# Layer 1's adaLN gate in two sums with three adding DMAs each, seven places for turned probabilities, and a new written order for the first layer

## The chip, the cores and the metric

The kernel runs on one core of a Trainium2 chip. A core has five engines, each with an instruction queue of its own: TensorE (PE, matrix products, with the loading of its stationary operand shown apart as PEld), VectorE (DVE), ScalarE (ACT), GpSimd (POOL) and SyncE (SP, which here only issues DMAs). The metric is the device time of one execution in microseconds (us). The kernel before took 416.38 us as the median of 3 runs (416.04 to 417.29).

## The reference

A decoder trunk of two layers on one sequence of 256 rows of 1024 numbers, all float32:

```
for i in range(DEPTH):                                   # DEPTH = 2
    shift, scale, gate = split(c @ ada_w[i] + ada_b[i], 3)
    h = rmsnorm(x, norm_g[i]) * (1 + scale) + shift
    y = nsa_mixer(h, ...) if i % 2 == 0 else mlstm_mixer(h, ...)
    x = x + gate * y
return rmsnorm(x, final_g)
```

Layer 1's mixer is sparse attention with 16 heads of 64 in 4 groups. It has a branch on compressed tokens (a small network with a hidden layer and a GELU over blocks of 32 rows), a branch on selected blocks and a sliding window; each has an ALiBi slope, a softmax and a sigmoid gate. With 256 rows there are four blocks of 64 and 16 to be selected, so the selection takes all that are allowed. The sum of the branches is multiplied by SiLU(z), called the path below, and goes through an output projection. Layer 2's mixer is a chunkwise mLSTM with 8 heads. The change is in layer 1 and in the turn from it to layer 2. The gate of layer 1 is one row of 1024 numbers: the 1024 numbers of c times a 1024 x 1024 block of ada_w, plus a third of ada_b.

## The kernel before, in words

Products that need full precision are made of three matmuls: each operand is split into a rounded part (hi, named wh or hh) and the rest (lo, named wl or hl), and hi x hi, hi x lo and lo x hi are added up in a bank of PSUM. ACT makes the hi of a loaded tile (L169), DVE its lo (L174). Loads come as tiles of up to 128 x 1024 in ten places named raw, issued by SP (L86) in a fixed order as soon as a place is free.

Layer 1 has an order of its own. Its first phase (0 to about 53 us) makes the modulated input and the first projections. What follows, to the start of layer 2, is driven by a string of step names, ORDER (L638 to L655): `attention` (L659) runs through the names and calls for each a small function that issues the step's instructions, on whatever engines it needs. Inside this block the scheduler leaves every engine, PE, ACT, DVE, POOL and SP, in the order in which the instructions were issued. So one sequence of names fixes the order on five engines. Layer 2 is ordered by a scheduler of the language, apart from a few stretches.

The names that matter here, with n for a pair of heads or a tile, and the lines of the functions:

- `hi`, `lo`: the two parts of the next weight tile. `k:kk,part`: products for the keys, values and branch gates. `E`: part of the embedding of positions. `hidden:n`: sixteen matmuls of the compression's hidden layer (L597).
- `S:n,a`, `m:n,a`, `e:n,a`, `f:n`: the scores (PE, L795 and L798), their minima with the mask (DVE, L814), the exponentials (ACT, L821) and the scaling factors (DVE, L829).
- `sXY:n,j`: the scaling of the probabilities. X and Y name the engine for each of the two branches: v for DVE, a for ACT, p for POOL. Each branch is two instructions, of 128x256 and 128x128 (L838, on ACT L665).
- `T:n,j,br`, `t:n,j,br`: three transposes of probabilities on PE (L843), and their copy from PSUM to a tile PT by ACT (L665). PT has eight places. `V:n`: the products of values with PT (L860). `C:n`: the compressed branch's products (L865). `y`, `Y`: the product with the path and its parts, into tiles Q. `z:n,q`: a quarter of the path's projection (L1611 to L1613).
- `gp:k`, `ga:k`: the gate's products. The 1024 rows of ada_w's block come as eight raw tiles k = 0 to 7 of 128 rows. `gp:0` (L888) scales tile 0 on ACT by c's numbers into a tile gate; `gp:k` scales tile k in its own place. `ga:0` adds the row of ada_b to gate's first row with a DMA that POOL issues. `ga:k` for k = 1 to 7 (L896) first copies one column of gate to a tile called seen, on POOL, which waits for the DMA before, and then issues a DMA that adds the scaled tile onto gate (L902). After the seven, `gs` (L905) sums gate's 128 rows with four matmuls against a column of ones (L908), `gc` copies the result (ACT), `g4` stores it to DRAM (POOL, L916), and `g5` (L918) reads it back, spread over all 128 rows, into gate (L919).
- `d:s,n`: shift and scale of layer 2, from raw tiles (L886).
- `out:n`, `l:a,half,k`: the output projection. `l` issues the three products of one Q tile with one weight tile, for one row block a and one half of the columns (L925). Three names make nine matmuls.
- `r:a,half`, `rp:a,half`: the residual x + gate * y of a row block and half, with the product on DVE (L1121) and the addition on DVE or POOL (L1122).
- The turn into layer 2, for row block a: `sq` (squares, ACT, L1155), `sc` (inverse root, DVE), `x:a,half` (normalised rows, ACT L1164 or DVE L1162), `tr:a,k4` (four transposes, PE, L1170), `md:a,k4` (scale and shift; the first half on ACT, L1181, the second on DVE, L1179), `ro:a,k4` (the rounded part; the first half on DVE, L1188, the second on ACT, L1186), `re:a,k4` (the rest, DVE, L1192), `n:a,m` (products with layer 2's narrow weights, L1201, one of the three products for each m) and `v:m,n` (products with its first wide weights, L1201). `nh` and `nl` are hi and lo for these.

The dependencies that the string must respect are those of the functions: `tr` needs `x`, `md` needs `tr`, `ro` needs `md`, `n:0,0` needs `ro:0,0` and then `ro:0,1`.

Of the kernel before, what the change touches and what calls it, by code (L numbers as in the profile page):

```python
# [23 lines left out]
class Kernel:  # L24
# [613 lines left out]
    ORDER = """  # L638
    gp:0 hi lo k:0,0 k:0,1 k:0,2 hi k:1,0 k:1,1 k:1,2 k:2,2 lo k:3,2 hi hi lo k:4,2 hi lo lo k:2,1 E:1,0 k:3,1 k:2,0 k:4,1 E:0,0 hi lo k:5,2 k:6,2
    k:3,0 k:4,0 k:5,0 k:6,0 k:7,0 qa:1 qa:3 qb:3 d:0,0 qb:1 hidden:0 gp:1 E:1,1 hi E:0,1 ga:0 hidden:1 ga:1 gp:2 qa:2 qb:2 k:7,2 kd qa:0 k:5,1 G:0  # L640
    qb:0 G:1 vo:0 hi lo hidden:2 lo S:0,0 hidden:3 hi m:0,0 e:0,0 gelu:0 S:0,1 m:0,1 e:0,1 gelu:1 lo z:0,0 gp:3 S:1,0 ga:2 f:0 vo:1 gelu:2 z:0,1
    sap:0,0 S:1,1 m:1,0 k:6,1 d:0,1 k:7,1 hi ga:3 turned z:0,2 vo:2 second m:1,1 T:0,0,1 T:0,0,0 z:0,3 spp:0,1 e:1,0 ckeys e:1,1 t:0,0,0 cvalues:0
    S:2,0 t:0,0,1 cscores:0 lo cscores:1 f:1 spa:1,0 cvalues:1 params d:0,2 zt:0 S:2,1 T:1,0,1 ccopy:0 ccopy:1 ctokens:0 T:0,1,0 t:1,0,1 zo:0 d:0,3 hi
    gp:4 T:0,1,1 t:0,1,1 t:0,1,0 hi z:1,0 z:1,1 ctokens:1 T:1,0,0 m:2,0 e:2,0 t:1,0,0 z:1,2 cdist:0 z:1,3 lo d:1,0 m:2,1 e:2,1 zt:1 cdist:1 cexp ga:4
    spp:1,1 f:2 spp:2,0 S:3,0 zo:1 T:1,1,1 T:1,1,0 gp:5 m:3,0 t:1,1,0 S:3,1 m:3,1 V:0 cprobs t:1,1,1 d:1,1 e:3,0 hi hi cparts:1 cparts:0 V:1 svp:2,1
    S:4,0 S:4,1 T:2,0,0 T:2,0,1 t:2,0,1 t:2,0,0 e:3,1 z:2,0 cturned:0 lo T:2,1,1 T:2,1,0 lo ga:5 z:2,1 t:2,1,1 cpt:0 z:2,2 t:2,1,0 cturned:1 f:3
    spa:3,0 C:0 m:4,0 T:3,0,1 T:3,0,0 m:4,1 z:2,3 e:4,0 e:4,1 t:3,0,0 y:0 V:2 d:1,2 f:4 spp:3,1 T:3,1,0 lo S:5,0 S:5,1 gp:6 ga:6 t:3,0,1 t:3,1,0 hi
    T:3,1,1 t:3,1,1 d:1,3 m:5,0 e:5,0 svp:4,0 zt:2 m:5,1 e:5,1 zo:2 V:3 S:6,0 T:4,0,0 t:4,0,0 T:4,0,1 C:1 S:6,1 y:1 z:3,0 spp:4,1 d:2,0 T:4,1,0
    t:4,0,1 f:5 cpt:1 spv:5,0 T:4,1,1 z:3,1 z:3,2 m:6,0 spv:5,1 m:6,1 t:4,1,0 hi gp:7 t:4,1,1 e:6,0 ga:7 hi lo d:2,1 T:5,0,0 z:3,3 T:5,0,1 V:4 lo C:2
    t:5,0,0 t:5,0,1 S:7,0 T:5,1,1 T:5,1,0 lo Y:0 e:6,1 t:5,1,0 f:6 S:7,1 m:7,0 m:7,1 t:5,1,1 spa:6,0 zt:3 zo:3 Y:1 sap:6,1 hi V:5 out:0 T:6,0,1 d:2,2  # L650
    d:2,3 T:6,1,0 gs out:1 l:1,1,2 d:3,0 e:7,0 e:7,1 f:7 lo l:1,0,2 y:2 t:6,0,1 t:6,1,0 gc d:3,1 T:6,1,1 T:6,0,0 l:0,0,2 d:3,2 l:0,0,3 g4 g5 saa:7,1
    sva:7,0 t:6,0,0 t:6,1,1 hi d:3,3 T:7,1,0 T:7,0,1 lo t:7,1,0 t:7,0,1 hi lo l:0,1,2 T:7,0,0 t:7,0,0 T:7,1,1 t:7,1,1 V:6 V:7 C:3 Y:2 l:0,0,4 l:0,1,3
    y:3 hi l:0,1,4 lo Y:3 hi l:0,1,5 l:0,0,5 l:0,0,6 lo l:0,0,7 l:0,1,6 l:0,1,7 l:1,0,3 nh:3 nl:3 r:0,0 l:1,1,3 l:1,0,4 l:1,1,4 root l:1,0,5 r:0,1
    nh:0 nh:1 sq:0,0 sq:0,1 nl:0 sc:0 x:0,1 nl:1 l:1,0,6 l:1,0,7 rp:1,0 nh:4 x:0,0 tr:0,0 nh:2 md:0,0 tr:0,1 md:0,1 ro:0,1 l:1,1,5 l:1,1,6 l:1,1,7
    ro:0,0 sq:1,0 nl:2 n:0,0 n:0,1 r:1,1 sq:1,1 re:0,0 re:0,1 sc:1 x:1,1 nh:5 nl:4 v:0,0 v:0,1 v:1,0 v:1,1 n:0,2 x:1,0 tr:1,0 md:1,0 tr:1,1 md:1,1  # L655
    v:2,0 v:2,1 ro:1,0 re:1,0 ro:1,1 re:1,1 nl:5 v:0,2 v:1,2 n:1,0 n:1,1 n:1,2 gt:0 gt:1
    """

    def attention(self, blocks):  # L659
# [183 lines left out]
                nc.tensor.transpose(b[:, k * P : k * P + P], st[n][0][j][:, br, k * P : k * P + P], ident)  # L843
# [51 lines left out]

        def gate_add(k):  # L896
            if not k:
                nc.gpsimd.dma_start(self.gate0[0:1], t["ada_b"][0:1, 2048:3072], accum_op=OP.add)
# [2 lines left out]
            nc.gpsimd.tensor_copy(T([P, 1], tag="seen"), self.gate0[:, 0:1])
            nc.gpsimd.dma_start(self.gate0, raw, accum_op=OP.add)  # L902
            self.used.add(n)

        def gate_sum():  # L905
            b = B["gs"] = self.bank(4)
            for j in range(4):
                nc.tensor.matmul(b[32 * j : 32 * j + 32, 0:256], self.ones1.to_broadcast([P, 32]), self.gate0[:, 256 * j : 256 * j + 256], start=True, stop=True, skip_group_check=True, tile_position=(0, 32 * j))  # L908
# [788 lines left out]
```

## Time and profile before

| | us |
|---|---|
| median of 3 timed runs | 416.38 (416.04 to 417.29) |
| profiled execution, its own time | 416.69 |
| its span in the profile | 414.9 |
| time of that execution outside the span | 1.8 |
| granted TensorE clock | 0.998 of full |
| first phase of layer 1 | 0 to about 53 |
| ORDER's stretch | about 53 to 176 |
| rest of layer 2 | 176 to 409 |
| end | 409 to 414.9 |

The profile shows one execution. Its first part gives the busy time of each engine and its share of the span; the chain follows the work that ended last back from the end and says which engine each step of it was on. Views of the trace give busy times in stretches of time (the windows), the instructions in order of time (the timeline, where neighbours of one kind are merged, and where the brackets say how long the engine sat idle before and what ended that), groups of instructions by line and shape, the waits by who waited for whom, and DMAs with the time from issue to landing. Ends of matmuls are modelled, so starts are the surer figures there. "bank" is a bank of PSUM, and "out<-in" names what an instruction writes and reads.

### The profile page before, as it was taken

The page shows a single profiled execution, that of the slowest core. Times are in us where ns is not written, and L with a number is a line of the kernel's source. Part 1 is how long each engine was busy: PE and PEld are TensorE (multiplying, and loading weights), DVE is VectorE, ACT ScalarE, POOL GpSimd, SP SyncE. Part 2 cuts the span into 40 slices and gives each one's busy share as a digit, 9 for nine tenths or more (in the row PEclk, how much of TensorE's full clock was granted, in tenths as well). Part 3 has the DMA queues.
Part 4 walks back from the last instruction along what each step waited for, and adds up shares of the span by engine and source line. Part 5 has one row for each costly group of instructions (what it writes and reads, how often), then busy time and mean ns, then how long its engine had stood idle before and what let it go on. Part 6 is the DMA issues. An engine that isn't in the chain of part 4 may idle for free.

```text
span 414.9 us, 7573 instructions
## 1 busy us (share of the span) xinstructions
PE 406.5 (98%) x2637; PEld 356.5 (86%) x2637; DVE 344.7 (83%) x721; ACT 278.9 (67%) x551; POOL 100.1 (24%) x176
## 2 busy tenths in 40 slices
PE   8999999999999999999999999999999999999994
PEld 5999998889889788888998999888888888888884
DVE  5999899899999989987873799998999766657653
ACT  5666696799999978776549866476366454464522
POOL 4000042286596300155205100001041210220000
PEclk9999999999999999999999999999999999999999
DMA  7999999999897988457684675756956646540002
GB/s 296 413 405 407 399 383 350 321 382 363 216 318 230 326 282 310 149 196 278 191 316 145 205 233 181 296 186 193 343 179 216 209 143 212 173 133 2 0 0 103
DMA packets 28967, 100.47 MB, mean 242 GB/s; under 512 B 3844, under 2 KB 4016, under 8 KB 28800
## 3 DMA queue, kind: packets, MB, share of 16 engines
q1 hardware_dynamic: 26208, 92.30, 62.2%
q0 software_dynamic: 2576, 7.41, 7.8%
q8 instruction: 21, 0.34, 0.3%
q10 hardware_dynamic: 144, 0.26, 0.2%
q14 instruction: 18, 0.15, 0.1%
HBM read 95.15 MB, written 1.13 MB: 232 GB/s over the span
## 4 chain that ended last, share of the span: by engine, by line
PE 92%; DMA 3%; DVE 2%; SPq 1%; ACT 1%; issue 1%; DVEq 0%
PE bank L562 10%; PE bank L564 10%; PE bank L563 10%; PE bank L439 7%; PE bank L1613 6%; PE bank L1611 6%; PE bank L1612 6%; PE bank L925 5%; PE bank L1529 5%; PE bank L1090 5%; PE bank L1201 4%; PE bank L860 3%; PE bank L843 3%; DMA raw<-in_start 3%; PE bank L1403 2%; PE bank L795 2%
## 5 line engine op out<-in xcount | busy, mean ns | idle before, releaser
L174 DVE TENSOR_TENSOR wl<-raw,wh 128x1024 fp32r<-128x1024 f32 (+3 forms) x118 | 138.8, 1192 | 32.8 <-ACT wh L169 30.3
L169 ACT ACTIVATE wh<-raw 128x1024 fp32r<-128x1024 f32 (+4 forms) x118 | 117.5, 1009 | 70.3 <-PE bank L564 31.3
L562 PE MATMUL bank<-wh,one 128*128 128x512 f32 (+2 forms) x208 | 76.9, 370 | 0.0
L563 PE MATMUL bank<-wl,one 128*128 128x512 f32 (+2 forms) x208 | 76.2, 367 | 0.0
L564 PE MATMUL bank<-wh,one 128*128 128x512 f32 (+2 forms) x208 | 76.0, 367 | 0.0
L1611 PE MATMUL bank<-one,wh 128*128 128x256 f32 x208 | 59.5, 286 | 0.0
L1613 PE MATMUL bank<-one,wl 128*128 128x256 f32 x208 | 58.9, 283 | 0.1
L1612 PE MATMUL bank<-one,wh 128*128 128x256 f32 x208 | 58.8, 283 | 0.0
L562 PEld LDWEIGHTS bank<-wh,one 128*128 128x128 f32 x208 | 39.2, 188 | 6.4 <-issue 0.4
L564 PEld LDWEIGHTS bank<-wh,one 128*128 128x128 f32 x208 | 39.2, 188 | 6.2
L563 PEld LDWEIGHTS bank<-wl,one 128*128 128x128 f32 x208 | 39.2, 188 | 5.9
L1613 PEld LDWEIGHTS bank<-one,wl 128*128 128x128 f32 x208 | 39.8, 191 | 0.3 <-DVE wl L174 0.3
L1612 PEld LDWEIGHTS bank<-one,wh 128*128 128x128 f32 x208 | 39.8, 191 | 0.2
L1611 PEld LDWEIGHTS bank<-one,wh 128*128 128x128 f32 x208 | 39.8, 191 | 0.2
L838 POOL TENSOR_SCALAR Pr<-Pr,f 128x128 f32<-128x128 f32 (+1 forms) x38 | 33.0, 923 | 19.8 <-DVE f L829 14.9
L439 PE MATMUL bank<-one,wh 128*128 128x256 f32 x224 | 29.9, 284 | 0.8 <-ACT one L413 0.3
L439 PEld LDWEIGHTS bank<-one,wh 128*128 128x128 f32 x224 | 28.0, 192 | 1.3 <-ACT wh L169 0.8
L821 ACT ACTIVATE Pr<-Pr,mn 128x128 f32<-128x128 f32 (+1 forms) x64 | 28.3, 453 | 0.0
L165 POOL TENSOR_TENSOR raw<-raw,gate 128x256 f32<-128x256 f32 x16 | 13.4, 840 | 53.2 <-DMA raw<-in_out_b 49.2
L1384 DVE SCALAR_TENSOR_TENSOR conv<-bank,one,conv 128x255 f32<-128x255 f32 (+2 forms) x48 | 20.5, 471 | 2.2 <-ACT conv L1379 2.2
L886 DVE CUSTOM_DVE_ANT_0 raw<-raw,one,one 128x1024 f32<-128x1024 f32 x16 | 20.8, 1316 | 0.0
L814 DVE CUSTOM_DVE_ANT_0 Pr<-bank,one 128x128 f32<-128x128 f32 (+1 forms) x64 | 18.7, 352 | 0.2
(351 smaller groups left out, 815.9 us busy)
## 6 DMA issues: line engine op xcount, KB each, us to landing
raw<-in_wide SPq DMA_DIRECT2D x44, 512.0 KB, 4.7
raw<-in_units SPq DMA_DIRECT2D x18, 512.0 KB, 4.4
raw<-in_turn SPq DMA_DIRECT2D x16, 512.0 KB, 7.4
raw<-in_out_b SPq DMA_DIRECT2D x16, 512.0 KB, 3.6
raw<-in_start SPq DMA_DIRECT2D x8, 512.0 KB, 9.6
Q<-in_columns SPq DMA_DIRECT2D x8, 512.0 KB, 9.6
raw<-in_gate SPq DMA_DIRECT2D x8, 512.0 KB, 9.1
raw<-in_hidden SPq DMA_DIRECT2D x8, 512.0 KB, 7.6
```

The costliest lines, as they stand in the source:

```text
L169: self.nc.scalar.activation(v(hi), src, AF.Copy)
L174: (g or self.nc.vector).tensor_tensor(v(lo), src, v(hi).bitcast(F32), op=OP.subtract)
L439: nc.tensor.matmul(out, w[:, ch * P : ch * P + P], h[:, kk], start=(kk == 0 and m == 0 and ch % 2 == 0), stop=(kk == 7 and m == 2), skip_g ...
L562: nc.tensor.matmul(out, self.hh[:, kk, sl], wh, start=first, stop=False, skip_group_check=True)
L563: nc.tensor.matmul(out, self.hh[:, kk, sl], wl, start=False, stop=False, skip_group_check=True)
L564: nc.tensor.matmul(out, self.hl[:, kk, sl], wh, start=False, stop=last, skip_group_check=True)
L821: nc.scalar.activation(v, v, AF.Exp, bias=mn[:, a, br, j : j + 1], scale=-1.0, accum_out=sm[:, a, br, j : j + 1])
L838: es[br].tensor_scalar(v, v, f, None, op0=OP.mult)
L886: nc.vector.tensor_tensor_reduce(raw, raw, self.cbc, scale, self.pca[:, 72 + 8 * b + kc : 73 + 8 * b + kc], OP.mult, OP.add, self.cols1[s] ...
L1611: nc.tensor.matmul(out, wh, self.hh[:, kk], start=first, stop=False, skip_group_check=skip)
L1612: nc.tensor.matmul(out, wh, self.hl[:, kk], start=False, stop=False, skip_group_check=skip)
L1613: nc.tensor.matmul(out, wl, self.hh[:, kk], start=False, stop=last, skip_group_check=skip)
```

## The change

The gate: `gp:0` and `gp:1` scale tiles 0 and 1 into two tiles, gate and a new gate2. Tiles 2 to 7 are added in turn, the even ones onto gate and the odd ones onto gate2, three DMAs each; the seen copy before each reads the sum that is added to. One adding DMA and one seen copy are gone. `gs` sums both tiles into the same bank with two matmuls for each quarter.

Memory: PT has seven places instead of eight. The column of ones and a column called sel become columns of the tile pca, and crep, a repeated copy of c's numbers, shares the place of a tile called zb; layer 2's gate sums read c's numbers from pca instead.

The order: ORDER is written anew from its first name to its last. The same steps stand in it, except that `ga:1` is gone, that one residual addition of the second row block is on POOL instead of DVE (`r:1,1` became `rp:1,1`), and that the letters of the scaling steps differ: of 32 branch scalings 5 were on DVE, 8 on ACT and 19 on POOL, and now 10, 5 and 17. Of the string only the lines with the gate sum and with the first transposes of the turn are shown.

```diff
-        self.sel = self.T(pc, [P, P])
+        self.sel = self.pca[:, 94:95]
...
-        self.ones1 = self.T(self.p1, [P, 1])
+        self.ones1 = self.pca[:, 95:96]
...
-        self.crep = self.T(pc, [P, KC, 32])
+        self.crep = self.T(p1, [P, KC, 32], tag="zb")
...
-    d:2,3 T:6,1,0 gs out:1 l:1,1,2 d:3,0 e:7,0 e:7,1 f:7 lo l:1,0,2 y:2 t:6,0,1 t:6,1,0 gc d:3,1 T:6,1,1 T:6,0,0 l:0,0,2 d:3,2 l:0,0,3 g4 g5 saa:7,1
...
-    nh:0 nh:1 sq:0,0 sq:0,1 nl:0 sc:0 x:0,1 nl:1 l:1,0,6 l:1,0,7 rp:1,0 nh:4 x:0,0 tr:0,0 nh:2 md:0,0 tr:0,1 md:0,1 ro:0,1 l:1,1,5 l:1,1,6 l:1,1,7
-    ro:0,0 sq:1,0 nl:2 n:0,0 n:0,1 r:1,1 sq:1,1 re:0,0 re:0,1 sc:1 x:1,1 nh:5 nl:4 v:0,0 v:0,1 v:1,0 v:1,1 n:0,2 x:1,0 tr:1,0 md:1,0 tr:1,1 md:1,1
...
+    hi V:4 S:7,0 C:2 T:5,0,0 t:5,0,0 zo:3 S:7,1 d:2,3 T:5,1,1 sap:6,1 lo m:7,0 m:7,1 gs t:5,1,1 V:5 T:6,1,1 hi Y:1 hi lo lo e:7,0 spv:6,0 e:7,1 gc g4
...
+    l:1,1,4 l:1,1,5 l:1,0,5 l:1,1,6 nl:2 sq:0,1 sc:0 x:0,0 l:1,1,7 rp:1,1 l:1,0,6 l:1,0,7 x:0,1 rp:1,0 tr:0,0 md:0,0 tr:0,1 md:0,1 ro:0,1 ro:0,0 nl:1
+    n:0,0 re:0,1 sq:1,0 sq:1,1 v:0,0 re:0,0 sc:1 x:1,1 n:0,1 n:0,2 nh:4 nl:4 v:0,1 x:1,0 tr:1,0 md:1,0 tr:1,1 md:1,1 ro:1,1 v:1,0 v:1,1 v:2,0 v:2,1
...
-            pt = PT[n, j, br] = T([P, 384], tag="PT", bufs=8)
+            pt = PT[n, j, br] = T([P, 384], tag="PT", bufs=7)
...
             if not k:
-                raw = self.take_raw(1)[0]
-                copy(self.gate0, raw, scale=self.pca[:, 0:1])
+                W["sums"] = [self.gate0, T([P, D], tag="gate2")]
+            if k < 2:
+                copy(W["sums"][k], self.take_raw(1)[0], scale=self.pca[:, k : k + 1])
                 return
...
-            nc.gpsimd.tensor_copy(T([P, 1], tag="seen"), self.gate0[:, 0:1])
-            nc.gpsimd.dma_start(self.gate0, raw, accum_op=OP.add)
+            nc.gpsimd.tensor_copy(T([P, 1], tag="seen"), W["sums"][k % 2][:, 0:1])
+            nc.gpsimd.dma_start(W["sums"][k % 2], raw, accum_op=OP.add)
...
-            for j in range(4):
-                nc.tensor.matmul(b[32 * j : 32 * j + 32, 0:256], self.ones1.to_broadcast([P, 32]), self.gate0[:, 256 * j : 256 * j + 256], start=True, stop=True, skip_group_check=True, tile_position=(0, 32 * j))
+            for m, w in enumerate(W["sums"]):
+                for j in range(4):
+                    nc.tensor.matmul(b[32 * j : 32 * j + 32, 0:256], self.ones1.to_broadcast([P, 32]), w[:, 256 * j : 256 * j + 256], start=(m == 0), stop=(m == 1), skip_group_check=True, tile_position=(0, 32 * j))
...
-            nc.vector.scalar_tensor_tensor(acc, raws[kc // 2][:, kc % 2], self.crep[:, kc, 0:1], src, op0=OP.mult, op1=OP.add)
+            nc.vector.scalar_tensor_tensor(acc, raws[kc // 2][:, kc % 2], self.pca[:, kc : kc + 1], src, op0=OP.mult, op1=OP.add)
```

More of the change, by code (lines that the diff above doesn't have):

```diff
@@ L638 @@
     ORDER = """
[L639 to L650, printed above, removed]
@@ L651 @@
-    d:2,3 T:6,1,0 gs out:1 l:1,1,2 d:3,0 e:7,0 e:7,1 f:7 lo l:1,0,2 y:2 t:6,0,1 t:6,1,0 gc d:3,1 T:6,1,1 T:6,0,0 l:0,0,2 d:3,2 l:0,0,3 g4 g5 saa:7,1
-    sva:7,0 t:6,0,0 t:6,1,1 hi d:3,3 T:7,1,0 T:7,0,1 lo t:7,1,0 t:7,0,1 hi lo l:0,1,2 T:7,0,0 t:7,0,0 T:7,1,1 t:7,1,1 V:6 V:7 C:3 Y:2 l:0,0,4 l:0,1,3
-    y:3 hi l:0,1,4 lo Y:3 hi l:0,1,5 l:0,0,5 l:0,0,6 lo l:0,0,7 l:0,1,6 l:0,1,7 l:1,0,3 nh:3 nl:3 r:0,0 l:1,1,3 l:1,0,4 l:1,1,4 root l:1,0,5 r:0,1
-    nh:0 nh:1 sq:0,0 sq:0,1 nl:0 sc:0 x:0,1 nl:1 l:1,0,6 l:1,0,7 rp:1,0 nh:4 x:0,0 tr:0,0 nh:2 md:0,0 tr:0,1 md:0,1 ro:0,1 l:1,1,5 l:1,1,6 l:1,1,7
@@ L655 @@
-    ro:0,0 sq:1,0 nl:2 n:0,0 n:0,1 r:1,1 sq:1,1 re:0,0 re:0,1 sc:1 x:1,1 nh:5 nl:4 v:0,0 v:0,1 v:1,0 v:1,1 n:0,2 x:1,0 tr:1,0 md:1,0 tr:1,1 md:1,1
-    v:2,0 v:2,1 ro:1,0 re:1,0 ro:1,1 re:1,1 nl:5 v:0,2 v:1,2 n:1,0 n:1,1 n:1,2 gt:0 gt:1
+    E:0,0 qa:0 hi hi hi gp:0 k:0,1 lo k:0,0 k:0,2 lo E:1,0 k:1,0 k:1,1 ga:0 hi k:1,2 k:2,1 k:2,0 k:3,0 hi k:2,2 k:3,2 lo hi hi lo lo lo lo k:4,0 qa:3
+    k:4,2 k:5,2 k:6,2 k:5,0 qb:3 E:0,1 qa:1 d:0,0 k:7,2 qa:2 k:6,0 gp:1 G:0 E:1,1 G:1 k:3,1 k:7,0 kd hidden:0 hidden:1 hidden:2 hidden:3 gp:3 qb:2
@@ new lines @@
+    qb:0 gp:2 hi qb:1 vo:0 ga:2 vo:1 S:0,0 k:4,1 S:0,1 gelu:0 m:0,0 e:0,0 gelu:1 m:0,1 k:5,1 gelu:2 e:0,1 S:1,0 m:1,0 S:1,1 f:0 e:1,0 lo turned z:0,0
+    m:1,1 d:0,1 ga:3 z:0,1 saa:0,0 T:0,0,0 d:0,2 k:6,1 k:7,1 second ckeys z:0,2 spp:0,1 e:1,1 vo:2 t:0,0,0 hi hi T:0,0,1 t:0,0,1 cscores:0 cscores:1
+    f:1 cvalues:0 lo T:0,1,1 S:2,0 S:2,1 hi cvalues:1 ccopy:1 t:0,1,1 ccopy:0 T:0,1,0 t:0,1,0 d:0,3 z:0,3 hi m:2,0 m:2,1 ctokens:0 ctokens:1 spp:1,1
+    T:1,1,0 zt:0 e:2,0 S:3,0 S:3,1 cdist:0 e:2,1 cdist:1 zo:0 t:1,1,0 cexp gp:4 params lo T:1,1,1 z:1,0 t:1,1,1 f:2 z:1,1 d:1,0 gp:5 cprobs z:1,2
@@ new lines @@
+    spp:1,0 T:1,0,1 T:1,0,0 d:1,1 spv:2,0 t:1,0,0 hi hi ga:4 z:1,3 V:0 spp:2,1 t:1,0,1 V:1 m:3,0 cparts:0 m:3,1 ga:5 T:2,0,1 cparts:1 zt:1 T:2,1,0
+    S:4,0 S:4,1 zo:1 e:3,0 lo t:2,1,0 t:2,0,1 cturned:0 T:2,0,0 e:3,1 T:2,1,1 lo z:2,0 t:2,1,1 f:3 m:4,0 svp:3,0 z:2,1 z:2,2 m:4,1 T:3,0,1 S:5,0 cpt:0
+    e:4,0 C:0 t:2,0,0 e:4,1 T:3,0,0 t:3,0,0 S:5,1 spv:3,1 d:1,2 t:3,0,1 f:4 spv:4,0 z:2,3 gp:7 T:3,1,0 T:3,1,1 gp:6 y:0 lo m:5,0 m:5,1 cturned:1 zt:2
+    V:2 svp:4,1 zo:2 t:3,1,0 d:1,3 t:3,1,1 V:3 lo d:2,0 hi e:5,0 C:1 y:1 T:4,0,1 e:5,1 z:3,0 T:4,0,0 t:4,0,0 S:6,0 t:4,0,1 S:6,1 T:4,1,0 t:4,1,0 ga:6
@@ new lines @@
+    T:4,1,1 t:4,1,1 f:5 sva:5,1 m:6,0 e:6,0 m:6,1 Y:0 d:2,1 d:2,2 z:3,1 z:3,2 ga:7 T:5,1,0 t:5,1,0 cpt:1 e:6,1 f:6 spp:5,0 z:3,3 zt:3 T:5,0,1 t:5,0,1
+    hi V:4 S:7,0 C:2 T:5,0,0 t:5,0,0 zo:3 S:7,1 d:2,3 T:5,1,1 sap:6,1 lo m:7,0 m:7,1 gs t:5,1,1 V:5 T:6,1,1 hi Y:1 hi lo lo e:7,0 spv:6,0 e:7,1 gc g4
+    out:0 T:6,1,0 t:6,1,0 out:1 lo l:0,0,2 f:7 t:6,1,1 d:3,0 svv:7,0 T:6,0,1 g5 t:6,0,1 T:6,0,0 t:6,0,0 y:2 d:3,1 l:0,0,3 sav:7,1 d:3,2 l:0,1,2
+    l:0,1,3 hi hi T:7,0,0 t:7,0,0 T:7,0,1 l:1,1,2 lo t:7,0,1 l:1,0,2 l:1,1,3 lo hi lo T:7,1,0 t:7,1,0 l:1,0,3 T:7,1,1 Y:2 V:6 d:3,3 t:7,1,1 V:7 C:3
@@ new lines @@
+    y:3 nh:3 l:0,1,4 hi lo nh:2 l:1,0,4 Y:3 l:0,1,5 l:0,0,4 l:0,0,5 l:0,0,6 nl:3 l:0,0,7 nh:0 nl:0 nh:1 l:0,1,6 l:0,1,7 root r:0,0 sq:0,0 r:0,1
+    l:1,1,4 l:1,1,5 l:1,0,5 l:1,1,6 nl:2 sq:0,1 sc:0 x:0,0 l:1,1,7 rp:1,1 l:1,0,6 l:1,0,7 x:0,1 rp:1,0 tr:0,0 md:0,0 tr:0,1 md:0,1 ro:0,1 ro:0,0 nl:1
+    n:0,0 re:0,1 sq:1,0 sq:1,1 v:0,0 re:0,0 sc:1 x:1,1 n:0,1 n:0,2 nh:4 nl:4 v:0,1 x:1,0 tr:1,0 md:1,0 tr:1,1 md:1,1 ro:1,1 v:1,0 v:1,1 v:2,0 v:2,1
+    ro:1,0 re:1,0 n:1,0 n:1,1 re:1,1 nh:5 nl:5 n:1,2 gt:0 v:0,2 gt:1 v:1,2
```

## Prediction

> **What bounds the kernel now.** I read the page first: the busy times and the chain that ended last.
>
> ```profile
> PE 406.5 (98%) x2637; PEld 356.5 (86%) x2637; DVE 344.7 (83%) x721; ACT 278.9 (67%) x551; POOL 100.1 (24%) x176
> PE 92%; DMA 3%; DVE 2%; SPq 1%; ACT 1%; issue 1%; DVEq 0%
> ```
>
> TensorE (PE) is busy for 98% of the span and is 92% of the chain. Whatever adds work or idle time to PE lengthens the kernel; whatever shortens another engine does nothing unless PE waits for that engine. An average hides stages, so the next view is the busy time by stage, for the stretch that the change rewrites (53 to 176 us) and the rest of layer 2 behind it. The columns behind the length are PE, PEld, DVE, ACT, POOL, then the granted clock, the DMA share and GB/s.
>
> ```profile
> 53.00:82.00 29.00, 28.88 (x226) 24.96 (x226) 26.05 (x52) 22.15 (x40) 7.87 (x14) 1.00 1.02 349
> 82.00:152.00 70.00, 69.96 (x569) 60.22 (x568) 68.67 (x221) 68.12 (x204) 41.92 (x54) 1.00 0.93 304
> 152.00:176.00 24.00, 23.94 (x138) 19.81 (x135) 21.35 (x45) 18.07 (x34) 1.29 (x1) 1.00 0.68 238
> 176.00:409.00 233.00, 233.00 (x1319) 204.58 (x1320) 181.52 (x323) 135.54 (x217) 40.61 (x71) 1.00 0.55 182
> ```
>
> Two things stand here. PE is full in every stage, and full to the digit from 176 to 409 us, so nothing lost before 176 us can be caught up later. And in 82 to 152 us three engines are nearly full together: PE 69.96, DVE 68.67 and ACT 68.12 of 70 us. Since the ends of matmuls are modelled, small gaps hide in that busy time; the chain, which goes from start to start, shows them (start, length, what, records):
>
> ```profile
> 68.93 3.60 PE bank L597 x32
> ...
> 88.03 0.80 PE bank L843 x6
> ...
> 95.03 0.66 PE bank L843 x6
> ...
> 118.96 0.48 PE bank L843 x3
> ...
> 120.84 0.33 PE bank L843 x3
> ...
> 136.57 1.45 PE bank L860 x16
> 138.03 3.00 PE bank L925 x12
> ...
> 141.68 0.57 PE bank L908 x8
> 142.25 4.40 PE bank L925 x18
> ...
> 154.13 11.12 PE bank L925 x48
> 165.26 0.87 PE bank L1170 x8
> 166.13 2.08 PE bank L925 x9
> 168.21 4.90 PE bank L1201 x32
> 173.11 0.87 PE bank L1170 x8
> 173.98 1.83 PE bank L1201 x8
> ```
>
> An undisturbed run of output products (L925) takes 11.12/48 = 0.232 us each. Eighteen would take 4.17 and took 4.40; twelve would take 2.78 and took 3.00. Three transposes of L843 take 0.33, once 0.48; six take 0.66, once 0.80. These four excesses come to 0.23 + 0.22 + 0.15 + 0.14 = 0.74 us. I allow as much again for runs that I do not quote, 1.5 us in all: that is the most that a better order of the same work could win before 176 us.
>
> **The gate in two sums.** The old gate sum is four matmuls of which the trace has eight records, 0.57 us. The new one has four more of the same shape. On PE at this step before (the L843 are transposed probabilities, gate the sum, the L925 output products):
>
> ```order
> L843 MATMUL bank_428_2113<-one_13_14_87,Pr_386_1934 128x128 [waits Activation_49] x2
> L843 MATMUL bank_428_2113<-one_13_14_87,Pr_386_1934 128x128
> L908 MATMUL bank_429_2117<-gate_165_813,one_22_23_101 32x256 [waits DMASW4_49,DMASW3_49,DVE_49]
> L908 MATMUL bank_429_2117<-gate_165_813,one_22_23_101 32x256 x3
> L925 MATMUL bank_421_2089<-wh_388_1949,Q_207_1052 128x512
> ```
>
> And now, on PE at the same step (gate2 is the second sum, the L860 are head 5's values):
>
> ```order
> L843 MATMUL bank_404_2036<-one_13_14_87,Pr_353_1779 128x128 x2
> L910 MATMUL bank_410_2061<-gate_160_811,one_7_8_72 32x256 [waits DMASW4_49,DMASW1_49,DVE_49]
> L910 MATMUL bank_410_2061<-gate_160_811,one_7_8_72 32x256 x3
> L910 MATMUL bank_410_2061<-gate2_171_828,one_7_8_72 32x256 [waits DMASW2_49]
> L910 MATMUL bank_410_2061<-gate2_171_828,one_7_8_72 32x256 x3
> L860 MATMUL bank_396_2002<-PT_403_2028,one_154_155_808 64x256 [waits Activation_49]
> ```
>
> The two rows with gate2 are new work on the full engine, **+0.57 us**, and the sum has moved ahead of head 5's values. The price is 0.57/8 = 0.071 us per record. The Trainium skill ("TensorE: Matmul & The Clock Gate", Back-to-back issue gap) gives N/2.4 + 2.5 ns between matmuls, 109 ns for 256 columns; by it the addition would be an estimated 0.87 us and the sum 0.3 more. The row decides against that, and the page's Part 3, on small matmuls that overlap in groups of columns, fits the row.
>
> What do the shorter chains of adding DMAs give back? First the time to landing by kind of DMA, then POOL's waits from 53 to 175 us, then the last adding DMA, the write-back and the first use of the gate in order of time:
>
> ```profile
> gate<-raw POOLq DMA_DIRECT2D x7, 512.0 KB, 8.6
> ...
> gate<-whole POOLq DMA_DIRECT2D x1, 512.0 KB, 7.0
> ...
> POOL seen L901 <- DMA gate<-raw: 0.9, 1, 0.9
> ...
> 132.07 0.91 POOL L902 DMA_DIRECT2D gate<-raw  x1 [0.30 <-POOL seen L901]
> ...
> 148.69 0.58 POOL L919 DMA_DIRECT2D gate<-whole  x1 [3.37 <-DMA whole<-adaA]
> 159.05 0.69 DVE L1121 TENSOR_TENSOR y<-bank,gate 128x512 f32<-128x512 f32 x1 [0.17 <-PE bank L925]
> ```
>
> POOL waited 0.9 us in all for an earlier adding DMA, and POOL is not what PE waits for. The last one was issued at 132.07 and landed about 132.98 + 8.6 = 141.6, just as the gate sum started (141.68). The finished gate was written back by about 149.27 + 7.0 = 156.3 and first used at 159.05. So one DMA and one seen copy less, and two chains instead of one, take nothing off PE except what the sum itself waited, 0.2 us at most (it lies in the 1.5 above). In the new order the sum stands ahead of head 5's values, which are the L860 of 136.57 in the chain, so near 136.7; the last product is scaled several steps earlier too, so that I put its adding DMA at 119 to 122 and its landing by 133. I cost the wait at nothing, with some 4 us of margin; if that margin goes, see the rivals.
>
> **The cover that goes.** This is the largest term. In the turn into layer 2, four instructions on other engines stand between the transposes of the new rows (L1170) and the first narrow product (L1201): two that scale and shift, two that round. ACT's half and DVE's half of them in the trace:
>
> ```profile
> 165.73 1.51 ACT L1181 ACTIVATE tz<-bank,cols 128x128 f32<-128x128 f32 x4 [0.71 <-PE bank L1170]
> 167.57 0.63 ACT L1186 ACTIVATE one<-tz 128x512 fp32r<-128x512 f32 x1 [0.33 <-DVE tz L1179]
> ...
> 173.58 1.50 ACT L1181 ACTIVATE tz<-bank,cols 128x128 f32<-128x128 f32 x4 [0.89 <-PE bank L1170]
> ```
>
> ```profile
> 166.17 1.37 DVE L1179 TENSOR_SCALAR tz<-bank,cols 128x128 f32<-128x128 f32 x4 [0.18 <-PE bank L1170]
> 167.45 0.42 DVE L1188 CAST one<-tz 128x512 fp32r<-128x512 f32 x1
> ...
> 175.31 0.41 DVE L1188 CAST one<-tz 128x512 fp32r<-128x512 f32 x1
> ```
>
> The transposes end at 165.26 + 0.87 = 166.13, and DVE's rounding at 167.45 + 0.42 = 167.87. PE cannot start L1201 for 1.74 us, and spent them on nine output products, 2.08 us. What stands on PE at this place before (bank_487 and bank_491 are the transposes, bank_424 the last output products, bank_496 the first narrow product):
>
> ```order
> L1170 MATMUL bank_491_2391<-one_13_14_87,Pr_477_2346 128x128 [waits DVE_49,PE_49]
> L1170 MATMUL bank_491_2391<-one_13_14_87,Pr_477_2346 128x128 x3
> L925 MATMUL bank_424_2092<-wh_455_2227,Q_206_1033 128x512
> L925 MATMUL bank_424_2092<-wl_456_2228,Q_206_1033 128x512
> L925 MATMUL bank_424_2092<-wh_455_2227,Q_206_1033 128x512
> L925 MATMUL bank_424_2092<-KL_425_2093,Q_194_986 128x512 x3
> L925 MATMUL bank_424_2092<-KH_426_2094,Q_194_986 128x512 x3
> L1201 MATMUL bank_496_2419<-wh_472_2337,one_3_4_70 128x272 [waits DVE_49,PE_49]
> ```
>
> And now (line numbers are two higher):
>
> ```order
> L927 MATMUL bank_424_2118<-KL_426_2120,Q_193_944 128x512 x3
> L927 MATMUL bank_424_2118<-KH_427_2121,Q_193_944 128x512 x3
> L1172 MATMUL bank_482_2388<-one_13_14_87,Pr_473_2340 128x128 [waits Activation_49]
> L1172 MATMUL bank_482_2388<-one_13_14_87,Pr_473_2340 128x128 x3
> L1172 MATMUL bank_484_2398<-one_13_14_87,Pr_475_2359 128x128 [waits DVE_49,PE_49]
> L1172 MATMUL bank_484_2398<-one_13_14_87,Pr_475_2359 128x128 x3
> L1203 MATMUL bank_489_2417<-wh_465_2320,one_3_4_70 128x272 [waits DVE_49,PE_49]
> ```
>
> All output products now stand ahead of the transposes, and nothing is between these and L1203. The nine products are not saved, only done earlier, so PE idles for the 1.74 us and a little for the signal: **+1.8 us**, bounds 1.7 (the rows above) and 2.4 (if a residual multiplication of 0.69 us, the 159.05 row, now stands just ahead of DVE's half). Queued behind the waiting product on PE is the whole of layer 2. At the second row block the cover stays: between its transposes (173.11 + 0.87 = 173.98) and DVE's rounding (175.31 + 0.41 = 175.72) lie 1.74 us, before with eight L1201 in 1.83 us, now with eight too (four steps). No cost there.
>
> **The rest of the new order.** Every row from 53 to 176 us changes its place; most of that has one answer, that PE does the same work in another sequence. Changes of kind between fp32 products (transposes and the like) and rounded ones rise by two round trips. The 18 and 12 products above cost 0.23 and 0.22 more than their rate, behind such a change; other runs show nothing: 0 to 0.46 us for two, I take **+0.2**. The scaling steps move between engines. One unit is a row of 128x256 and one of 128x128; grouped by shape:
>
> ```profile
> L838 POOL TENSOR_SCALAR Pr<-Pr,f 128x256 f32<-128x256 f32 x19 | 20.2, 1063 | 0.0
> L838 POOL TENSOR_SCALAR Pr<-Pr,f 128x128 f32<-128x128 f32 x19 | 14.9, 784 | 19.8 <-DVE f L829 14.9 <-ACT PT L665 3.6 <-ACT tz L756 1.3
> ...
> L665 ACT ACTIVATE Pr<-Pr,f 128x256 f32<-128x256 f32 x8 | 4.0, 500 | 0.0
> L665 ACT ACTIVATE Pr<-Pr,f 128x128 f32<-128x128 f32 x8 | 3.2, 396 | 0.4 <-DVE f L829 0.4
> ...
> L838 DVE TENSOR_SCALAR Pr<-Pr,f 128x256 f32<-128x256 f32 x5 | 2.2, 433 | 0.0
> L838 DVE TENSOR_SCALAR Pr<-Pr,f 128x128 f32<-128x128 f32 x5 | 2.1, 415 | 0.0
> ```
>
> Before, 5 units are on DVE, 8 on ACT, 19 on POOL; now 10, 5 and 17. DVE gains 5 x (0.43 + 0.42) = 4.2 us (less where two overlap), ACT loses 3 x 0.90 = 2.7, POOL 2 x 1.85 = 3.7. DVE runs behind PE's needs by a margin that differs from step to step; I follow its order and find it at most 1 us late at two scores and paths, and some old waits gone. I take 0 for all that, with -1.5 (the bound above) and +2.9 (DVE, below) as ends. Seven places for turned probabilities instead of eight, the constants in shared columns and the one residual addition that goes to POOL cost nothing that I see: their readers follow within a head, or, for the addition, some 4 us of PE work later.
>
> Sum: 0.57 + 0.2 + 1.8 + 0 = +2.6 us. The profiled execution took 416.69, with a span of 414.9, so 1.8 us lie outside, which the change does not touch: 419.3. The median of the timed runs is 0.3 lower: **419.0 us**.
>
> **Rivals.**
> *Not slower: the new order earns its gaps back.* If the small gaps between 53 and 152 us go, up to 1.5 us, and the change of kind costs nothing, the sum is 0.57 + 1.8 - 1.5 = +0.9, 417.3. The bound for "no change" is 0.3%, 1.25 us, about what a measurement of this kernel can tell; the point from which this decides is 1.1 to 1.3 us of gaps gone. For it: the order is new through all of the stretch. Against it: only 0.74 us of gaps can be pointed at. Chance 0.20. To be faster by 1.25 it would need the gaps gone and the lost cover at nothing as well, which the rows of the turn speak against: 0.08, about 415.0.
> *DVE becomes the bound.* It has 70 - 68.67 = 1.33 us idle in 82 to 152 us and gets up to 4.2 more: 2.9 us that PE would wait, 421.9; with half of them hidden, 420.5. For it: no idle time. Against it: ACT and POOL are relieved, and some of the steps may fall before 82 us, where DVE has 29 - 26.05 = 2.95 us. Chance 0.14.
> *A transfer comes late.* The new gate sum at 136.7 needs its last adding DMA issued by 136.7 - 0.9 - 8.6 = 127.2. If POOL reached it at the old 132.07, PE would wait 4.9 us: 423.9; half of it, 421.5. The eight hidden tiles, first used at 68.93, are used in one block now and could stall it likewise. Against it: the scaled product is ready earlier, and the tiles' loads stand ahead of two gate loads. Chance 0.08. The Trainium skill ("DMA: Bandwidth & Descriptors", Anatomy of one DMA) has 2.0 us plus bytes at 436 GB/s, an estimated 3.2 us for 512 KB; by that the deciding point would be 132.6 and I would give 0.03. The trace has 8.6 us, with the engines busy at 0.93, and decides.
>
> **Numbers.** My forecast (418.1 to 420.2) has 0.50, the rivals 0.20, 0.08, 0.14 and 0.08. Its own range is -0.9 and +1.2 about 419.0: 0.6 of unseen gaps and 0.3 of changes of kind below, 0.6 of cover, 0.3 of changes of kind and 0.3 of DVE above. The range for 8 in 10 takes in "no change" down to 416.3 and DVE up to 421.6, and leaves out the faster case and the worst of the late ones. Faster by over 0.3%: 0.08; within: 0.20; slower: 0.72.
>
> **What would show it.** Right: in the trace after, PE idle of 1.7 to 2.4 us just before the first L1203, released by DVE's rounding; the gate sum with 16 records in 1.1 us, not waiting for a DMA; layer 2 from there to the end of the same length. Wrong: L1203 starting within 0.5 us of the transposes' end; or a start of the turn's transposes more than 1.5 us earlier than the sum says (the gaps earned), or later, with waits for DVE's scaled probabilities or for a DMA at the gate sum or at L597.

## The result and the profile after

The changed kernel takes 419.5 us (median of 4 runs, 419.18 to 420.83) against 416.56 in the same series: a ratio of 1.0069, 95% interval 1.0052 to 1.0086. It is slower by 2.9 us; the forecast was 2.6. The profiled execution took 419.18 with a span of 417.4, 2.5 us over the span before. Four executions in the series below that took 500 us or more are not counted.

The busy times of the page of the changed kernel:

```profile
PE 406.0 (97%) x2645; PEld 356.2 (85%) x2645; DVE 343.4 (82%) x730; ACT 278.6 (67%) x545; POOL 95.0 (23%) x171
...
PE 82%; DVE 8%; DMA 4%; ACT 2%; issue 2%; SPq 1%; DVEq 0%
```

PE has eight records more and no more busy time; the span grew by idle time. The last line is the chain's. The stages of the changed kernel (length, then PE, PEld, DVE, ACT, POOL, granted clock, DMA share, GB/s) say where:

```profile
53.00:82.00 29.00, 27.94 (x218) 24.19 (x218) 25.81 (x57) 24.06 (x45) 7.94 (x17) 1.00 0.99 365
82.00:152.00 70.00, 69.88 (x569) 60.81 (x567) 68.53 (x219) 64.52 (x189) 38.44 (x44) 1.00 0.89 282
152.00:178.50 26.50, 24.56 (x151) 20.20 (x150) 23.98 (x48) 18.66 (x36) 2.68 (x2) 1.00 0.65 231
178.50:412.00 233.50, 233.33 (x1319) 204.56 (x1317) 178.40 (x322) 135.96 (x218) 37.26 (x71) 1.00 0.54 181
```

PE lacks 1.94 us in the stretch of the turn, 1.06 between 53 and 82 us, and nothing to speak of elsewhere. PE's own waits in the changed kernel (total, times, longest) name both; the second did not exist before:

```profile
PE bank L1203 <- DVE one L1190: 1.9, 1, 1.9
...
PE bank L795 <- DVE mn L814: 0.9, 1, 0.9
```

And its chain shows the gate sum, and the turn where the cover had been:

```profile
136.80 1.00 PE bank L910 x16
...
139.73 2.80 PE bank L927 x12
...
142.86 3.51 PE bank L927 x15
...
156.63 11.07 PE bank L927 x48
167.71 0.89 PE bank L1172 x8
168.62 1.36 DVE tz L1181 x4
169.98 0.34 DVE one L1190
...
170.46 4.17 PE bank L1203 x28
174.64 0.87 PE bank L1172 x8
175.51 1.83 PE bank L1203 x8
```

The chain leaves PE for DVE's scaling and rounding, exactly the two instructions that nine L925 had covered. The account goes by starts. These are the last eight products of the first phase, the turn's transposes and the first narrow products on PE, in the kernel before and in the changed one:

```profile
52.09 1.12 PE L439 MATMUL bank<-one,wh 128*128 128x256 f32 x8
...
165.09 1.04 PE L1170 MATMUL bank<-one,Pr 128*128 128x128 f32 x8
...
168.05 1.20 PE L1201 MATMUL bank<-wh,one 128*128 128x272 f32 x8
```

```profile
51.69 1.12 PE L439 MATMUL bank<-one,wh 128*128 128x256 f32 x8
...
167.54 1.04 PE L1172 MATMUL bank<-one,Pr 128*128 128x128 f32 x8
170.46 1.71 PE L1203 MATMUL bank<-wh,one 128*128 128x272 f32 x10 [1.89 <-DVE one L1190]
```

The transposes start 2.45 us later than before, but the nine products (2.08) now lie ahead of them, so PE is 0.37 late for the same work. It had begun ORDER's stretch 0.40 early. That is no gain of the order: the same eight products start at 51.50 and 52.62 in two kernels below that run the first phase of the kernel before. So PE lost 0.77 inside the stretch: 0.43 for the gate sum (1.00 against 0.57) and 0.93 for the new wait, less 0.59 that other gaps gave back. Then comes the hole. From the transposes' start to the first narrow product there were 2.96 us with 2.08 of products in them, and there are 2.92 without: 2.04 us lost, of which 1.89 shows as idle time. The narrow products start 2.41 us late, and from there to the end both kernels take the same time to 0.1 us.

### The profile page after: what moved, and what is told of

Same layout as the page of the kernel before. It is cut to its first block, busy times and chain, and to the rows that moved or that the text cites. A ratio compares the mean times of both kernels' runs of the same rounds, so it can differ in the third digit from the quotient of the medians.

```text
span 417.4 us, 7575 instructions
## 1 busy us (share of the span) xinstructions
PE 406.0 (97%) x2645; PEld 356.2 (85%) x2645; DVE 343.4 (82%) x730; ACT 278.6 (67%) x545; POOL 95.0 (23%) x171
## 4 chain that ended last, share of the span: by engine, by line
PE 82%; DVE 8%; DMA 4%; ACT 2%; issue 2%; SPq 1%; DVEq 0%
PE bank L564 10%; PE bank L562 10%; PE bank L563 10%; PE bank L439 7%; PE bank L927 5%; PE bank L1531 5%; PE bank L1092 5%; PE bank L1615 5%; PE bank L1613 5%; PE bank L1614 5%; PE bank L1203 4%; DMA raw<-in_start 2%; PE bank L1405 2%; PE bank L860 2%; PE bank L843 2%
## 5 line engine op out<-in xcount | busy, mean ns | idle before, releaser
L174 DVE TENSOR_TENSOR wl<-raw,wh 128x1024 fp32r<-128x1024 f32 (+4 forms) x118 | 136.4, 1174 | 30.2 <-ACT wh L169 29.0
L169 ACT ACTIVATE wh<-raw 128x1024 fp32r<-128x1024 f32 (+3 forms) x118 | 116.8, 1007 | 62.2 <-PE bank L564 27.0
```

What stands on the lines that cost most here:

```text
L169: self.nc.scalar.activation(v(hi), src, AF.Copy)
L174: (g or self.nc.vector).tensor_tensor(v(lo), src, v(hi).bitcast(F32), op=OP.subtract)
```

## The experiments

The theory after the result: the lost cover is the loss; the gate sum costs its matmuls; the new wait is a local accident of the order. The first rival: the cover's loss is absorbed. The second: what the shorter gate chains give, which the prediction had put at nothing.

**The cover taken from the kernel before.**

```diff
-    nl:1 l:1,0,6 l:1,0,7 rp:1,0 nh:4 x:0,0 tr:0,0 nh:2 md:0,0 tr:0,1 md:0,1 ro:0,1 l:1,1,5 l:1,1,6 l:1,1,7
+    nl:1 l:1,0,6 l:1,0,7 rp:1,0 nh:4 x:0,0 l:1,1,5 l:1,1,6 l:1,1,7 tr:0,0 nh:2 md:0,0 tr:0,1 md:0,1 ro:0,1
```

> The kernel before with one edit: the nine output products that stood between the transposes of the turn and the first narrow product now stand ahead of the transposes. Lost cover (my theory): PE idles 1.7 to 1.9 us before the first L1201, released by DVE's rounding, and the kernel takes 1.8 us more, about 418.2 to 418.4. Rival, the loss is absorbed (PE catches up in layer 2, or the chain to the transposes had slack): at most 0.3 us more, 416.4 to 416.7.

420.52 us against 417.02, ratio 1.0083 (1.0070 to 1.0097): 3.5 us, twice what was expected. The wait was the expected one. What follows it was not. PE's order of time in this kernel, and the windows of 2 us over the place:

```profile
170.52 2.01 PE L1201 MATMUL bank<-wh,one 128*128 128x272 f32 x8 [1.89 <-DVE one L1188]
172.32 1.97 PE L1201 MATMUL bank<-wl,one 128*128 128x272 f32 x8
```

```profile
170.00:172.00 2.00, 1.48 (x7) 1.51 (x8) 1.97 (x5) 1.24 (x3) 0.00 (x0) 0.67 0.00 0
172.00:174.00 2.00, 2.00 (x11) 2.00 (x10) 1.97 (x7) 1.60 (x4) 0.00 (x0) 0.50 0.75 260
174.00:176.00 2.00, 2.00 (x11) 1.67 (x11) 1.89 (x5) 1.09 (x2) 0.00 (x0) 0.98 0.01 2
```

Eight products take 2.0 us instead of the 1.2 that they took in the kernel before: the granted clock fell to half right behind the idle time. The losses of the three windows are 0.66 + 1.00 + 0.04 = 1.7 us of clock, so half clock lasted 3.4 us. 1.89 + 1.7 = 3.6 is close to the measured 3.5. Here all four executions had a granted clock of 0.993 or 0.994. In the changed kernel's profiled execution the same idle time had no such effect.

**Less of the cover taken.**

```diff
-    nh:4 x:0,0 tr:0,0 nh:2 md:0,0 tr:0,1 md:0,1 ro:0,1 l:1,1,5 l:1,1,6 l:1,1,7
+    nh:4 x:0,0 l:1,1,5 l:1,1,6 tr:0,0 nh:2 md:0,0 tr:0,1 md:0,1 ro:0,1 l:1,1,7
```

> The kernel before with six of the nine covering matmuls moved ahead of the transposes, three left (0.7 us of cover). The wait in L1201's place is then 1.89 - 0.70 = 1.2 us. If each us of idle PE costs one us: 1.2 us more than before. If the granted clock falls whenever PE idles at this place: 1.2 + 1.7 = 2.9 us more, clock 0.994 or less. If it falls only after more than about half of a stretch of 3.4 us idle: 1.2 us more, with the clock at 0.997 or above in every execution.

418.69 against 416.96, ratio 1.0033 (1.0021 to 1.0046), 1.4 us. The clock was 0.997 or above in every execution compared, so the third case holds. PE's waits of this kernel:

```profile
PE bank L1201 <- DVE one L1188: 1.2, 1, 1.2
```

**The changed kernel once more**, for its clock.

> The changed kernel itself, for the granted clock of more executions. One of its four showed 0.993 and 1.3 us more. If the drop after the idle 1.9 us depends on where in the clock's own stretches the idle time falls: a part of the executions, between 1 in 5 and 1 in 2, with 0.993 to 0.995 and 1.2 to 1.7 us above the others. If that one was a chance of something else: none. The ratio to before: 1.006 to 1.008.

420.43 against 417.06, ratio 1.0078 (1.0059 to 1.0096). Three of six executions showed 0.994 or 0.995 and took 421.04 to 421.35; the others 419.42 to 419.82. So the lost cover costs about 2 us always, and about 1.5 us more in some executions.

**The cover given back to the changed kernel.** From head 7's values on, the old order's end is used; l:1,1,3, l:1,0,3 and l:1,0,4 go behind l:0,1,7, which lets three later products stand behind the transposes.

```diff
-    lo t:7,0,1 l:1,0,2 l:1,1,3 lo hi lo T:7,1,0 t:7,1,0 l:1,0,3 T:7,1,1 Y:2 V:6 d:3,3 t:7,1,1 V:7 C:3
+    lo t:7,0,1 l:1,0,2 lo hi lo T:7,1,0 t:7,1,0 T:7,1,1 Y:2 V:6 t:7,1,1 V:7 C:3
...
+    rp:1,0 nh:4 x:0,0 tr:0,0 nh:2 md:0,0 tr:0,1 md:0,1 ro:0,1 l:1,1,5 l:1,1,6 l:1,1,7
```

> The changed kernel with the end of the old order from head 7's values on: three products of the second row block move from before these values to behind the residual, so that nine matmuls stand again between the turn's transposes and the first narrow product. If the lost cover costs what its wait shows: 1.9 us less than the changed kernel, 417.3 to 417.8, and no execution with a granted clock of 0.994 or less. Rival, DVE is behind with the heavier share of scalings and had needed these products as cover earlier: waits before L843, L860 or L1172 take 0.5 us or more of it back, 418.0 to 419.0.

418.15 against 416.96, ratio 1.0018 (0.9999 to 1.0037); 0.5% under the changed kernel's 1.0069, some 2.1 us by the ratios. The 418.15 by itself is above the 417.3 to 417.8 expected, in the rival's band; but the kernel before ran 0.4 us above the 416.56 of the first series here, and the rival's waits before L843, L860 or L1172 are not in the trace. So the ratio decides. No execution compared had a clock below 0.997. Its chain has the cover again:

```profile
165.87 0.87 PE bank L1172 x8
166.74 2.09 PE bank L927 x9
168.83 5.04 PE bank L1203 x32
```

**The new wait at 79 us.** In the changed kernel ACT waits for a gate tile, whose load stands behind eight hidden tiles, and all that ACT does next is late:

```profile
ACT raw L665 <- DMA raw<-in_gate: 4.1, 1, 4.1
```

Two edits tried to remove PE's 0.93. The first puts m:0,1 ahead of gelu:1:

```diff
-    gelu:0 m:0,0 e:0,0 gelu:1 m:0,1 k:5,1 gelu:2 e:0,1
+    gelu:0 m:0,0 e:0,0 m:0,1 gelu:1 k:5,1 gelu:2 e:0,1
```

> The changed kernel with one pair of steps swapped: on DVE the second minima of the first heads (m:0,1) stand ahead of the GELU's second step, which waits for ACT. In the changed kernel PE waited 0.93 us at 79 us for these minima. If that wait is DVE's order alone: it goes, 418.5 to 418.8. Rival, the late gate tiles hold ACT and DVE there in any order, and the wait moves on to the next scores or to the turned GELU: 419.2 to 419.5.

The second puts the gate tiles later, and loads the path's tile ahead of them:

```diff
-    hidden:3 gp:3 qb:2 qb:0 gp:2 hi qb:1 vo:0 ga:2 vo:1 S:0,0 k:4,1 S:0,1 gelu:0 m:0,0 e:0,0 gelu:1 m:0,1 k:5,1 gelu:2 e:0,1 S:1,0 m:1,0 S:1,1
+    hidden:3 qb:2 qb:0 qb:1 vo:0 vo:1 S:0,0 k:4,1 S:0,1 hi gelu:0 m:0,0 e:0,0 gelu:1 gp:3 m:0,1 k:5,1 gelu:2 e:0,1 S:1,0 m:1,0 gp:2 S:1,1 ga:2
```

> The changed kernel with the scaling of gate tiles 3 and 2 on ACT, and with that their loads, moved behind the GELU's first step, and the next weight's hi ahead of them. In the changed kernel ACT waited 4.08 us for these tiles, and PE 0.93 us behind that at 79 us. If the late tiles are the cause: ACT's wait and PE's go, 418.4 to 418.8. Rival, the wait only moves, as it did when the GELU's step was put later: 419.2 to 419.6.

Neither paid: 1.0065 (1.0051 to 1.0079) and 1.0051 (1.0032 to 1.0070), the changed kernel's own ratio within the intervals. The wait moved. In the first it stands at the turned GELU:

```profile
PE bank L694 <- DVE y L689: 0.8, 1, 0.8
```

and in the second at the first transposes, behind ACT's scaling of the first probabilities (PE in order of time):

```profile
84.85 0.84 PE L843 MATMUL bank<-one,Pr 128*128 128x128 f32 x3 [1.32 <-ACT Pr L665]
```

So for this wait the rival held. Both edits together, with the cover back:

> The edits of the two runs before together. If both prices are real and add up: 419.5 - 1.9 - 0.9 = 416.7, and 416.2 to 417.2 with the spread; that is the kernel before plus 0.43 us of gate matmuls less the gaps that the shorter gate chains removed in the old order. Rival, DVE's lateness: 417.5 to 418.5.

417.63 against 416.96, ratio 1.0010 (0.9999 to 1.0020). The time lies in the rival's band, the ratio also in that of the sum (416.2 to 417.2 over 416.56 is 0.9991 to 1.0015). The cover's part is there. The wait's part is not shown: the median is 0.5 us under that of the cover alone, but in the traces PE waits 1.3 us before L843 in place of 0.7 before L795, and from the last eight products of the first phase to the turn's transposes both kernels take the same 113.9 us.

**The new code in the old order.** The changed kernel with the ORDER of before, less `ga:1`; run twice.

> The changed kernel's code (two sums, seven places for turned probabilities, shared columns) with the old order less the one adding DMA that is gone. My theory: the four added matmuls cost 0.43 us (1.00 us after against 0.57 before) and nothing else changes: 416.8 to 417.0. Rival, the shorter chains of adding DMAs pay for them because the gate sum had waited: 416.4 to 416.6. Rival, seven places make PE wait: 417.5 or more, with waits before L860 or L843.

> The changed kernel's code with the old order less one adding DMA once more, as the reference for the two runs beside it and as the fastest version so far: 0.998 of before, 0.997 to 0.999.

416.32 against 417.02, ratio 0.9983 (0.9972 to 0.9994), and again 416.41 against 417.06, 0.9980 (0.9969 to 0.9991). It is the fastest complete version and beats both kernels: about 0.7 us come from the code, against its 0.43 of matmuls. So about 1.1 us came back, 0.7 to 1.7 by the intervals. PE waits nowhere before L860 or L843, so seven places are enough in this order. Two kernels split what changed in the chains. One is the kernel before without the second tile's addition (a part of the gate is missing), with one sum; the other is the new code in the old order with all seven adding DMAs, and a POOL memset more:

```diff
+            if k == 1:
+                raw = self.take_raw(1)[0]
+                copy(raw, raw, scale=self.pca[:, k : k + 1])
+                return
...
-    hidden:1 ga:1 gp:2
+    hidden:1 gp:2
```

> The kernel before with the second gate tile scaled but not added (that part of the gate is left out): one sum, six adding DMAs, old order, eight places, no added matmuls. Two sums in the old order were 0.7 us faster than before although their matmuls cost 0.43, so about 1.1 us came back somewhere. If it comes from one DMA and one seen copy less on POOL: all of the 1.1 us shows here, about 0.997 of before. If it comes from the halved chains (a seen copy that no longer waits): at most 0.3 us, 0.999 to 1.000 of before.

```diff
                 W["sums"] = [self.gate0, T([P, D], tag="gate2")]
-            if k < 2:
-                copy(W["sums"][k], self.take_raw(1)[0], scale=self.pca[:, k : k + 1])
+                nc.gpsimd.memset(W["sums"][1], 0.0)
+                copy(W["sums"][k], self.take_raw(1)[0], scale=self.pca[:, k : k + 1])
                 return
...
-    hidden:1 gp:2
+    hidden:1 ga:1 gp:2
```

> Two sums in the old order with all seven adding DMAs kept: the second sum starts from a POOL memset and takes four, the first three. If one DMA less is the gain: it is lost, and the matmuls' 0.43 us stay, 1.000 to 1.002 of before. If the halved chains are the gain: 0.998 to 0.999 of before, as with six.

Six in one sum: 0.9981 (0.9969 to 0.9993), as good as two sums, though not the 0.997 expected. Seven in two sums: 1.0004 (0.9994 to 1.0015), the gain is gone. So it is the DMA less, not the halved chains. How it reaches PE is seen on ACT, at its hi of the next path tile. The kernel before, the seven in two sums, the six in two sums, and the six in one:

```profile
78.68 1.06 ACT L169 ACTIVATE wh<-raw 128x1024 fp32r<-128x1024 f32 x1 [3.07 <-DMA raw<-in_path]
```

```profile
78.50 1.06 ACT L169 ACTIVATE wh<-raw 128x1024 fp32r<-128x1024 f32 x1 [3.27 <-DMA raw<-in_path]
```

```profile
75.53 1.06 ACT L169 ACTIVATE wh<-raw 128x1024 fp32r<-128x1024 f32 x1 [0.63 <-DMA raw<-in_path]
```

```profile
76.61 1.06 ACT L169 ACTIVATE wh<-raw 128x1024 fp32r<-128x1024 f32 x1 [0.76 <-DMA raw<-in_path]
```

With seven ACT waits 3 us for the load, with six 0.7, and the exponentials behind it start earlier. The load comes earlier for two reasons, as SP's issue of it shows, in the kernel before and with six in two sums:

```profile
72.55 0.33 SPq L86 DMA_DIRECT2D raw<-in_path  x1
```

```profile
71.09 0.38 SPq L86 DMA_DIRECT2D raw<-in_path  x1
```

Of the 3.15 us by which ACT's hi starts earlier (78.68 against 75.53), 1.46 lie ahead of the issue, because a place was free sooner, and 1.69 between issue and use, because the transfer was faster.

On PE the gain lies between the first products of the compression (L707) and the six transposes near 95 us, again before and with six in two sums:

```profile
87.03 0.56 PE L707 MATMUL bank<-adaA,PcT 128*128 128x64 f32 x4
...
94.87 0.83 PE L843 MATMUL bank<-one,Pr 128*128 128x128 f32 x6
```

```profile
86.87 0.56 PE L707 MATMUL bank<-adaA,PcT 128*128 128x64 f32 x4
...
94.03 0.92 PE L843 MATMUL bank<-one,Pr 128*128 128x128 f32 x6
```

From start to start that is 7.84 and 7.16 us. The other two kernels with six take 7.17 and 7.16; the others with seven take 8.01 (two sums), 7.62 and 7.92 (the two with less cover, which are the kernel before up to here). So the traces place 0.5 to 0.8 us of the gain; the rest of the 1.1 is not placed. That the way from the DMA to these products leads through ACT's wait is read from the order of the rows; no run shows it by itself.

**The new order with the old code.** One sum, seven adding DMAs, with `ga:1` put just ahead of `gp:2`; that place was my choice.

> The old code (one sum with seven adding DMAs, eight places) with the new order, and the seventh adding DMA put back. If the two sums only cost matmuls: 419.5 less 0.43, 419.1. What I expect instead: in the new order the last two adding DMAs are issued 1.5 us apart at 122.0 and 123.5; in one chain the last must wait until the one before has landed, 122.0 + 0.9 + 8.6 = 131.5, and lands near 141, while the gate sum stands at 136.8: PE waits 4 to 5 us there, 423 to 424.

430.04 against 417.02, ratio 1.0318 (1.0283 to 1.0353): 13 us, not 7, and not at the gate sum. Its waits from 50 to 150 us:

```profile
POOL seen L901 <- DMA gate<-raw: 24.0, 4, 9.3
...
DVE one L716 <- POOL one L711: 4.2, 1, 4.2
...
PE bank L733 <- DVE one L716: 4.0, 1, 4.0
...
PE bank L795 <- DVE mn L814: 2.2, 1, 2.2
...
PE bank L843 <- POOL Pr L838: 1.9, 3, 1.4
```

The seen copies stand on POOL's queue and wait up to 9.3 us for the DMA before; a memset queued behind them holds DVE, and DVE holds PE for 4.0 us. Its three waits in these rows, the 1.9 of the lost cover and the half clock, which comes twice for 3.4 us and costs 1.7 each time, make up 13.4 us. In one chain, adding DMAs may not stand as close together as this order has them. With the two sums they did not make PE wait, at these places.

## Why the prediction was right, and where it was not

- *The cover that goes*, +1.8: right in place, releaser and size (1.89 us of idle time, 2.04 from start to start), and shown by taking the cover from the kernel before (slower) and giving it back to the changed one (2.1 us faster). Too small in price: the half clock behind the idle time was not in the sum. It adds about 1.5 us in 1 of the first 4 and 3 of the next 6 executions of the changed kernel. The profiled execution had none of it.
- *The gate in two sums*, +0.57: the matmuls cost 0.43. But "take nothing off PE" is the step that failed. I followed the adding DMAs only along POOL and to the gate sum, and they did not bind there. The DMA that is gone lets a path tile land earlier, for which ACT waited 3 us, and behind that PE is 0.5 to 0.8 us faster. In the old order the new code is worth 0.7 us net, measured twice. What the missing DMA is worth in the new order was not separated.
- *The gate sum's margin*: right. The last adding DMA was issued at 123.52, which with the 8.6 us of the median lands by about 133; the sum started at 136.80 and waited for nothing.
- *The rest of the new order*, 0 taken, -1.5 and +2.9 as ends: the profiled execution shows 0.93 of new waiting and 0.59 of gaps gone, within the ends. The changes of kind, +0.2, did not show: at 11.07/48 = 0.231 us each, the 12 and 15 output products behind transposes would take 2.77 and 3.46 and took 2.80 and 3.51. The excesses of 0.22 and 0.23 on which that term rested are gone.
- *Rival, DVE becomes the bound*: did not happen as priced. DVE is busy 68.53 of 70 us with twice the scalings, and PE 69.88. But DVE has no room left there: the chain of the changed kernel lies on a path tile's load, ACT and DVE from 70.52 to 110.66, and PE's part of the chain falls from 92% to 82%. PE then waits only 0.12 us for DVE.
- *Rival, a transfer comes late*: a little of it did, at another place: 4.1 us on ACT for a gate tile, 0.93 on PE. I had looked at the hidden tiles, which had gone ahead, and not at the loads they went ahead of.
- *Rival, not slower*: 0.59 of gaps earned, where 1.1 to 1.3 would have decided.

That the sum came within 0.3 us is partly luck: 0.93 of unforeseen waiting stands against 0.59 of gaps gone and 0.2 that did not show.

## What to carry to other kernels

On a full engine, look for work that stands between a step and its own result on another engine: that work is cover, and moving it forward costs the whole chain that it hid. Price such a hole twice, its length and the half clock that may follow. And follow a removed DMA to the loads beside it and behind it, not only along its own queue.
